# Angle tables by doubling, six accumulator blocks held in PSUM, and expert products placed by hand behind the scores, in a two-layer streaming encoder

## The chip, the core and the metric

One core of a Trainium2 chip runs the whole program. TensorE (PE in the profile, with PEld its weight loads) multiplies, VectorE (DVE), ScalarE (ACT) and GpSimd (POOL) do the rest, SyncE (SP) issues most transfers. The metric is the device time of one execution in microseconds, the median of several.

## What is computed

For 576 tokens (512 of a prompt, 64 of a sample) each of two layers does:

- three token mixers side by side: a diagonal complex state-space layer (SSM), banded attention, and retention; then gates, an output projection and a layer norm;
- PEER: for 8 heads, scores against 2 x 128 sub-keys, the best 16 of each, the best 16 of their sums; these name rows of two tables of 16384 experts,

```
u = u_tab[ek]                                  # 128 chosen experts of a token
act = gelu(einsum('bhkd,bd->bhk', u, xk))
w = gate * act
out = einsum('bhk,bhkd->bd', w, v_tab[ek])
```

- a gated input embedding and a further layer norm.

The SSM turns its state by angles that grow with the token: it needs tables of cos and sin of (t+1) times theta, 128 x 576 each, for 8 groups of states in each layer.

## The kernel before, in words

Activations lie with features on the partitions and tokens along the row. Every product of a weight block and activations is made of three matmuls, high part by high, high by low and low by high (`mm3_steps`, L215); `weights` (L207) loads a 128x1024 block `wr` from SP's queue, ACT casts it to `wh` (L204) and DVE, or POOL where `eng=G` is given, subtracts to get `wl` (L205). There are 3 buffers of `wr` and 4 each of `wh` and `wl`.

A planner that comes with the language orders the instructions of each engine by its own model of times, with the order of the program as the priority. Inside `manual_schedule(engines={PE})` PE alone keeps the order of the program. Each engine then works through its list in order, and so does SP's queue, stores among it.

PSUM has 8 banks: `lin` 3, `bgd` 1, `aux` (`bank()`) 4.

**Mixers** (`mixers`, L399). The SSM, retention, projections and gates are woven by hand-made estimates (`weave`, L137). `rotation` (L419) makes the angle tables on POOL: six products and sums over 128x576 from two small tables, `rot` (16 wide) and `rot16` (36 wide), which the start of the program fills by doubling on DVE. In layer 0 the SSM calls it for 8 groups (`begin`, L708). The tables of layer 1 are also made in layer 0, by `next_tables` (L919) in the attention, and are stored to DRAM on SP's queue (L922); layer 1 loads them. Up to `GB` = 8 gate tiles are made ahead as filling.

**PEER** (`peer_ple`, L994). 160 tokens are served by gathering rows (POOL's indirect loads L1237, DVE's L1243 and L1255). The other 416 are served densely: all 128 blocks of 128 experts are multiplied, and the weight of every pair that was not chosen is zero. The stages are:

1. Scores and top 16 (`query`, `top16`, to L1097).
2. The softmax (L1099 to L1106) and the list turns: five calls of `to_slots` (L1109), each five PE transposes and a copy by ACT. Then the key look-ups (L1157 to L1165): 32 rounds, each a mask by DVE and, for two halves, a matmul by PE and a predicated copy by DVE.
3. `FR0` = 128 steps of u products. `hidden(i)` (L1009) makes the products of block i in 8 steps of three 128x416 matmuls into a `lin` bank, and ACT puts the gelu into an `act` tile. The generator `prefetch` (L1017) does this for `N_EARLY` = 34 blocks spread over the 128, which are stored to DRAM, and for the first 8, which stay. The FR0 steps are the first ones under `manual_schedule`; in these POOL makes `wl`.
4. One-hot stage (L1198): in 26 rounds DVE makes one-hot matrices, PE sums the gates of each expert and token (L1210, L1211) and makes 8 more steps of u products, ACT writes `gs`, and SP stores it to `gd`.
5. Expert loop (L1283): 64 rounds of `GE` = 2 blocks. A round makes or reloads the u products of two blocks, `LA` = 6 blocks ahead of use; it multiplies two `act` tiles by the gates `gblk` (L1302, every fourth block on POOL, the others on DVE), splits them into Wh and Wl, converts two v blocks, and makes 6 matmuls for each of 8 output blocks d (L1324). For d < `HELD` = 2 the sum stays in PSUM over all rounds; for the other six it goes to an `aux` bank and DVE adds it to `R[d]` (L1329). Steps of the gathered part are spread over the rounds (`advance`).

Of the kernel before, what the change touches and what calls it, by code (L numbers as in the profile page):

```python
# [23 lines left out]
T = 576  # L24
TP = 512
# [24 lines left out]
N_EARLY = 34  # L50

GB = 8
# [10 lines left out]
FR0 = 128  # L63
# [5 lines left out]
GG = 4  # L69

HELD = 2
# [84 lines left out]
def body(ctx, tc, nc, A, O, depth=DEPTH, dbg=None):  # L156
# [156 lines left out]
    rot16 = [cst.tile([128, nst, 36], F32, name=f"rq{i}") for i in range(2)]  # L313
    with ExitStack() as c0:
# [58 lines left out]
        for i in range(2):  # L373
            V.memset(rot16[i][:, :, 0:1], 1.0 - i)
            V.tensor_copy(rot16[i][:, :, 1:2], rot[i][:, :, 15:16])
        for m in (1, 2, 4, 8, 16):
            double(V, rot16[0], rot16[1], 1, m)
        for i in range(2):
            V.tensor_copy(rot16[i][:, :, 32:36], rot16[i][:, :, 0:4])
# [19 lines left out]
def mixers(tc, env):  # L399
# [6 lines left out]
    with ExitStack() as c:  # L406
# [4 lines left out]
        o36 = lambda t: t.rearrange("p (a b) -> p a b", b=16)  # L411
# [7 lines left out]
        def rotation(qq, pl, bufs):  # L419

            new = lambda n, b=1: pl.tile([128, T], F32, name=n, bufs=b)
            ct, sn, tx = new("ct", bufs), new("sn", bufs), new("tx")
            c1 = [e.rot16[i][:, qq, :, None].to_broadcast([128, 36, 16]) for i in range(2)]
            c2 = [e.rot[i][:, qq, None, :].to_broadcast([128, 36, 16]) for i in range(2)]
            G.tensor_mul(o36(ct), c1[0], c2[0])
            G.tensor_mul(o36(tx), c1[1], c2[1])
            G.tensor_sub(ct, ct, tx)
            tx = new("tx")
            G.tensor_mul(o36(sn), c1[0], c2[1])
            G.tensor_mul(o36(tx), c1[1], c2[0])  # L430
            G.tensor_add(sn, sn, tx)
            return ct, sn
# [256 lines left out]
        def ssm():  # L689
# [18 lines left out]
            def begin(q):  # L708
# [4 lines left out]
                else:  # L713
                    ct, st = rotation(q, sp, 2)
# [114 lines left out]
        with ExitStack() as ca:  # L829
# [89 lines left out]
            def next_tables():  # L919
                for q in range(8):  # L920
                    for i, t in enumerate(rotation(L * 8 + 8 + q, pa, 1)):
                        SY.dma_start(e.tables[q, i], t)  # L922
                    yield
# [70 lines left out]
def peer_ple(tc, env):  # L994
# [8 lines left out]
    with ExitStack() as c:  # L1003
# [24 lines left out]
        fill = prefetch()  # L1028
        with ExitStack() as cr:
# [7 lines left out]
            with ExitStack() as ck:  # L1037
# [60 lines left out]

                ex = tk.tile([128, 5, 8, 16], F32, name="ex")  # L1099
# [9 lines left out]
                def to_slots(src, dst):  # L1109
# [5 lines left out]
                    S.copy(dst[:, TP:], p1[:, :64])  # L1115

# [40 lines left out]
                for dst, src, pos in ((IT, LT[0], aT), (JT, LT[1], bT)):  # L1157
                    V.memset(dst, 0.0)
                    for a in range(16):
                        mk = tk.tile([128, T], U16, name="mk", bufs=2)  # L1160
                        V.tensor_scalar(mk, pos, float(a), None, op0=OP.is_equal)
                        for lo, hi in HALF:
                            p = bank()
                            PE.matmul(p[:, :HF], sel[:, a], src[:, lo:hi], start=True, stop=True)
                            V.copy_predicated(dst[:, lo:hi], mk[:, lo:hi], p[:, :HF])  # L1165
                twice(I2, IT)
# [26 lines left out]
            man = ExitStack()  # L1193
# [270 lines left out]
```

## Time and profile before

| | us |
|---|---|
| median of 3 runs (4280.81, 4293.08, 4308.05) | 4293.08 |
| the profiled execution | 4261.82 |
| its span, first to last instruction | 4260.0 |
| granted TensorE clock, share of full | 0.974 |

A row of a view of stretches reads: start:end, its length, then for each engine its busy time and (x) the number of instructions begun, then the share of the clock that was granted, the mean busy share of the 16 DMA engines, and GB/s. A row of grouped instructions reads: line, engine, operation, out<-in, shapes, xcount | busy us, mean ns of one | idle time before them and what ended it. A row of waits reads: who waited <- for whom: us in total, times, the longest.

### The profile page before, as it was taken

What the parts mean: (1) busy time and instruction counts of PE and PEld (TensorE: products, weight loads), DVE (VectorE), ACT (ScalarE), POOL (GpSimd) and SP (SyncE); (2) the same over time, 40 slices, a digit from 0 to 9 for tenths busy, and PEclk for the clock granted to TensorE, in tenths of its full rate; (3) what the DMA queues carried; (4) which work ended last, traced back from release to release, by engine and by line L of the source; (5) the groups of instructions that cost most, each with busy time, mean ns of one, the idle gap of its engine ahead of it and who ended that gap; (6) DMA issues with size and microseconds to landing.
All of it is one profiled execution on the core that took longest, in us unless ns stands there. A gap on an engine that the chain in (4) does not pass through costs nothing.

```text
span 4260.0 us, 65840 instructions
## 1 busy us (share of the span) xinstructions
PE 4050.0 (95%) x25032; PEld 3789.8 (89%) x25032; DVE 3433.5 (81%) x6827; ACT 1562.5 (37%) x2600; POOL 1435.8 (34%) x1050
## 2 busy tenths in 40 slices
PE   6998999898999999999999999999989999999998
PEld 6787899798999999999787889897989999999997
DVE  8944459987999989999678344698979999999985
ACT  3223433376333333333432243333843333233324
POOL 4634123301545445443100011332035444454421
PEclk8999999999999999999999999999999999999999
DMA  3123222277998989898232222124789999889961
GB/s 114 56 76 113 67 72 79 96 262 266 321 336 315 330 297 331 302 336 283 68 99 83 83 85 78 60 81 137 282 287 331 322 327 317 311 310 321 320 210 43
DMA packets 353886, 873.78 MB, mean 205 GB/s; under 512 B 33184, under 2 KB 169504, under 8 KB 350240
## 3 DMA queue, kind: packets, MB, share of 16 engines
q1 hardware_dynamic: 261408, 533.98, 36.4%
q0 software_dynamic: 92160, 335.59, 22.1%
q8 instruction: 196, 3.21, 0.3%
q14 instruction: 122, 1.00, 0.1%
HBM read 788.09 MB, written 79.00 MB: 204 GB/s over the span
## 4 chain that ended last, share of the span: by engine, by line
PE 71%; DVE 15%; DMA 7%; POOL 3%; issue 2%; ACT 1%; SPq 0%; POOLq 0%; DVEq 0%; ACTq 0%
PE lin L221 38%; PE aux L1324 16%; DMA wr<-in_uT 3%; PE lin L1324 3%; PE bgd L1324 3%; PE aux L221 2%; PE aux L132 2%; DVE wl L205 1%; DVE s L1052 1%; DVE t L132 1%; PE aux L265 1%; PE aux L1210 1%; PE aux L1211 1%; DMA gr<-in_u,gidx 1%; DVE hi L132 1%
## 5 line engine op out<-in xcount | busy, mean ns | idle before, releaser
L221 PE MATMUL lin<-XH,wh 128*128 128x288 f32 (+1 forms) x4288 | 1411.9, 330 | 25.1 <-ACT wh L204 13.7
L221 PE MATMUL lin<-XH,wl 128*128 128x288 f32 (+1 forms) x4288 | 1392.8, 325 | 9.5 <-DVE wl L205 9.5
L221 PE MATMUL lin<-XL,wh 128*128 128x288 f32 (+1 forms) x4288 | 1396.3, 326 | 0.0
L204 ACT CAST wh<-wr 128x1024 fp32r<-128x1024 f32 x692 | 713.0, 1047 | 1861.8 <-PE aux L1324 675.6
L205 DVE TENSOR_TENSOR wl<-wr,wh 128x1024 fp32r<-128x1024 f32 x628 | 784.0, 1264 | 379.8 <-ACT wh L204 309.1
L221 PEld LDWEIGHTS lin<-XH,wh 128*128 128x128 f32 x4288 | 815.3, 190 | 65.2 <-issue 29.2
L221 PEld LDWEIGHTS lin<-XH,wl 128*128 128x128 f32 x4288 | 814.4, 190 | 18.3 <-DVE wl L205 10.5
L221 PEld LDWEIGHTS lin<-XL,wh 128*128 128x128 f32 x4288 | 815.7, 190 | 12.1 <-issue 7.3
L1324 PE MATMUL aux<-Wh,wh 128*128 128x416 f32 (+1 forms) x1560 | 552.0, 354 | 36.1 <-DVE R L1329 36.1
L1324 PE MATMUL aux<-Wh,wl 128*128 128x416 f32 (+1 forms) x1560 | 550.0, 353 | 0.0
L1237 POOL DMA_INDIRECT gr<-in_v,gidx x320 | 426.7, 1333 | 364.7 <-DVE gr L1243 215.4
L1237 POOL DMA_INDIRECT gr<-in_u,gidx x320 | 414.5, 1295 | 374.2 <-DVE acc L1255 214.5
L1329 DVE TENSOR_TENSOR R<-R,aux 128x416 f32<-128x416 f32 x780 | 426.0, 571 | 18.5 <-PE aux L1324 17.1
L1255 DVE SCALAR_TENSOR_TENSOR acc<-gr,wg,acc 128x1024 f32<-128x1024 f32 x316 | 407.6, 1290 | 12.1 <-DMA gr<-in_v,gidx 12.0
L1243 DVE SCALAR_TENSOR_TENSOR gr<-gr,xtok 128x1024 f32<-128x1024 f32 x320 | 406.1, 1272 | 10.0 <-DMA gr<-in_u,gidx 9.9
L1324 PEld LDWEIGHTS aux<-Wh,wh 128*128 128x128 f32 x1560 | 295.7, 190 | 45.8 <-DVE R L1329 45.2
L1302 POOL TENSOR_TENSOR act<-act,gblk 128x416 f32<-128x416 f32 x64 | 96.4, 1507 | 636.5 <-DMA gblk<-gd 453.2
L1324 PEld LDWEIGHTS aux<-Wh,wl 128*128 128x128 f32 x1560 | 295.8, 190 | 3.7
L1324 PE MATMUL aux<-gr,wh 128*128 128x416 f32 x780 | 272.8, 350 | 0.0
L1324 PE MATMUL aux<-Wl,wh 128*128 128x416 f32 x780 | 272.1, 349 | 0.0
L205 POOL TENSOR_TENSOR wl<-wr,wh 128x1024 fp32r<-128x1024 f32 x64 | 155.5, 2430 | 323.0 <-ACT wh L204 272.6
L1212 ACT ACTIVATE gs<-aux 128x512 f32<-128x512 f32 x208 | 206.7, 1166 | 0.0
(405 smaller groups left out, 5937.2 us busy)
## 6 DMA issues: line engine op xcount, KB each, us to landing
wr<-in_uT SPq DMA_DIRECT2D x256, 512.0 KB
wr<-in_v SPq DMA_DIRECT2D x256, 512.0 KB
gd<-gs SPq DMA_DIRECT2D x26, 2048.0 KB
gblk<-gd SPq DMA_DIRECT2D x64, 832.0 KB
wr<-in_w_in SPq DMA_DIRECT2D x92, 512.0 KB
wr<-in_peer_wq SPq DMA_DIRECT2D x32, 512.0 KB
ad<-act SPq DMA_DIRECT2D x68, 208.0 KB
act<-ad SPq DMA_DIRECT2D x68, 208.0 KB
```

The source lines that it names most:

```text
L132: return f(out, *a, **k)
L204: S.copy(hi, src)
L205: (eng or V).tensor_sub(lo, src, hi)
L221: PE.matmul(out[:, :b - a], wt[:, s], x[:, a:b], start=(first and k == 0 and g == 0), stop=(last and k == n - 1 and g == 2))
L265: PE.matmul(var[:1, :HF], ones1, sq, start=(d == 0), stop=(d == ND - 1))
L1212: S.activation(gs[:, :, o + t:o + t + 4].rearrange("p i t -> p t i"), p.rearrange("p (t i) -> p t i", t=4), AF.Copy, scale=1.0 / GSCALE)
L1237: G.indirect_dma_start(out=r, out_offset=None, in_=A[table], in_offset=bass.IndirectOffsetOnAxis(ap=gidx[:, s:s + 1], axis=0))
L1243: V.scalar_tensor_tensor(r, r, 1.0, xtok[s // 128], op0=OP.mult, op1=OP.mult, accum_out=dots[:, s:s + 1])
L1255: V.scalar_tensor_tensor(o, r, w, o, op0=OP.mult, op1=OP.add)
L1302: (G if GG and i % GG == 0 else V).tensor_mul(a3, a3, gblk[:, :, i % IB])
L1324: PE.matmul(p, x[:, w], y[:, a - NG:b - NG], start=(j == 0 and g == 0 and (e0 == 0 or not hold)), stop=(j == GE - 1 and g == 2 and (fin or ...
L1329: V.tensor_add(R[d][:, a:b], R[d][:, a:b], p)
```

## The change

- `rot16` goes. `rotation` starts from `rot` and doubles: for m = 16, 32, 64, 128, 256 ACT makes two products of m columns with a scale, and DVE two combined multiply-adds that write the next m columns; two copies of 16 and two of 64 columns by ACT complete a pair of tables.
- `GB` is 10; `N_EARLY` is 38.
- PE keeps the order of the program from the last scores on. `FR0` goes; 48 steps of u products (`FH`) stand behind the scores, 4 (`FS`) behind each list turn, 1 behind each half of a look-up.
- `HELD` is 6: `bgd`, two `lin` and three `aux` banks hold d = 0 to 5 over the whole loop; one `lin` bank is left for u products and one `aux` bank for d = 6 and 7. These two are copied to SBUF by ACT, and DVE adds the copy.
- A round's order is d = 0, 1, 2, 6, 3, 4, 5, 7, its first u block ahead of it and its second before d = 3.
- All gate products (L1302) are on DVE.

```diff
-N_EARLY = 34
-GB = 8
+N_EARLY = 38
+GB = 10
-FR0 = 128
+FH = 48
+FS = 4
-GG = 4
-HELD = 2
+HELD = 6
+ORDER = (0, 1, 2, 6, 3, 4, 5, 7)
...
-        for i in range(2):
-            V.memset(rot16[i][:, :, 0:1], 1.0 - i)
-            V.tensor_copy(rot16[i][:, :, 1:2], rot[i][:, :, 15:16])
-        for m in (1, 2, 4, 8, 16):
-            double(V, rot16[0], rot16[1], 1, m)
-        for i in range(2):
-            V.tensor_copy(rot16[i][:, :, 32:36], rot16[i][:, :, 0:4])
...
-            G.tensor_mul(o36(ct), c1[0], c2[0])
-            G.tensor_mul(o36(tx), c1[1], c2[1])
-            G.tensor_sub(ct, ct, tx)
-            tx = new("tx")
-            G.tensor_mul(o36(sn), c1[0], c2[1])
-            G.tensor_mul(o36(tx), c1[1], c2[0])
-            G.tensor_add(sn, sn, tx)
+            c0, s0 = (r[:, qq] for r in e.rot)
+            S.copy(ct[:, :16], c0)
+            S.copy(sn[:, :16], s0)
+            m = 16
+            while m < TP:
+                c, s = (c0, s0) if m == 16 else (ct[:, :m], sn[:, :m])
+                cm, sm = c[:, m - 1:m], s[:, m - 1:m]
+                S.activation(tx[:, 0, :m], s, AF.Copy, scale=sm)
+                S.activation(tx[:, 1, :m], c, AF.Copy, scale=sm)
+                V.scalar_tensor_tensor(ct[:, m:2 * m], c, cm, tx[:, 0, :m], op0=OP.mult, op1=OP.subtract)
+                V.scalar_tensor_tensor(sn[:, m:2 * m], s, cm, tx[:, 1, :m], op0=OP.mult, op1=OP.add)
+                m *= 2
+            for t in (ct, sn):
+                S.copy(t[:, TP:], t[:, :T - TP])
...
+                man.enter_context(tc.manual_schedule(engines={mybir.EngineType.PE}))
+                run(fill, FH)
                 ex = tk.tile([128, 5, 8, 16], F32, name="ex")
...
                     S.copy(dst[:, TP:], p1[:, :64])
+                    run(fill, FS)
...
                             V.copy_predicated(dst[:, lo:hi], mk[:, lo:hi], p[:, :HF])
+                            run(fill, 1)
...
-            man = ExitStack()
-            man.enter_context(tc.manual_schedule(engines={mybir.EngineType.PE}))
-            run(fill, FR0)
...
-            for i in range(e1, min(e1 + GE, 128)):
-                if i in acts:
-                    continue
-                if i in early:
-                    acts[i] = ap_.tile([128, ND_T], F32, name="act", bufs=LA + GE)
-                    SY.dma_start(acts[i], ad[i])
-                else:
-                    run(hidden(i))
+            ahead = iter([i for i in range(e1, min(e1 + GE, 128)) if i not in acts])
+            def first_products(n):
+                for _, i in zip(range(n), ahead):
+                    if i in early:
+                        acts[i] = ap_.tile([128, ND_T], F32, name="act", bufs=LA + GE)
+                        SY.dma_start(acts[i], ad[i])
+                    else:
+                        run(hidden(i))
             e0 = e1 - LA
             if e0 < 0:
+                first_products(GE)
                 continue
+            first_products(1)
...
-                (G if GG and i % GG == 0 else V).tensor_mul(a3, a3, gblk[:, :, i % IB])
+                V.tensor_mul(a3, a3, gblk[:, :, i % IB])
...
-                held = [e.bgd(), lin()][:HELD]
+                held = [e.bgd(), lin(), lin(), bank(), bank(), bank()]
...
-                for d in range(ND):
+                for d in ORDER:
+                    if d == 3:
+                        first_products(GE)
...
+                    if not hold:
+                        t = lp.tile([128, ND_T], F32, name="vo", bufs=2)[:, :b - a]
+                        S.copy(t, p)
+                        p = t
                     V.tensor_add(R[d][:, a:b], R[d][:, a:b], p)
```

## Rows read from the trace of the kernel before

**Rows 1.** The page's first part: busy time of each engine.
```profile
PE 4050.0 (95%) x25032; PEld 3789.8 (89%) x25032; DVE 3433.5 (81%) x6827; ACT 1562.5 (37%) x2600; POOL 1435.8 (34%) x1050
```
**Rows 2.** Stretches: one-hot stage, gap, both expert loops, 50 us of the first.
```profile
863.00:1025.50 162.50, 162.50 (x1434) 155.81 (x1432) 140.08 (x120) 134.05 (x153) 0.00 (x0) 1.00 0.70 263
1025.50:1042.40 16.90, 0.11 (x2) 0.00 (x0) 5.90 (x9) 8.33 (x14) 1.83 (x2) 0.57 0.77 257
1042.40:2044.00 1001.60, 984.05 (x5187) 969.00 (x5188) 945.58 (x1319) 311.02 (x436) 470.21 (x351) 0.99 0.89 312
3136.90:4137.00 1000.10, 981.25 (x5186) 967.31 (x5187) 945.90 (x1319) 311.06 (x436) 463.85 (x351) 0.99 0.89 312
1450.00:1500.00 50.00, 50.00 (x266) 49.41 (x265) 49.09 (x68) 15.68 (x23) 23.84 (x18) 1.00 0.92 324
```
**Rows 3.** Waits of PE in the first expert loop.
```profile
PE aux L1324 <- DVE R L1329: 17.3, 12, 5.1
```
**Rows 4.** Waits of PE in the second expert loop.
```profile
PE aux L1324 <- DVE R L1329: 18.8, 12, 5.2
```
**Rows 5.** Grouped instructions of DVE in the first expert loop.
```profile
L205 DVE TENSOR_TENSOR wl<-wr,wh 128x1024 fp32r<-128x1024 f32 x212 | 253.7, 1218 | 33.2 <-ACT wh L204 32.3 <-PE aux L1324 0.5 <-issue 0.2
L1329 DVE TENSOR_TENSOR R<-R,aux 128x416 f32<-128x416 f32 (+2 forms) x389 | 212.6, 572 | 9.5 <-PE aux L1324 9.0
...
L1302 DVE TENSOR_TENSOR act<-act,gblk 128x416 f32<-128x416 f32 x96 | 57.4, 608 | 0.0
```
**Rows 6.** Grouped instructions of ACT in the first expert loop.
```profile
L1014 ACT ACTIVATE act<-lin 128x416 f32<-128x416 f32 x86 | 43.8, 509 | 0.0
L1246 ACT ACTIVATE wg<-dots 128x16 f32<-128x16 f32 x10 | 2.1, 213 | 20.8 <-DVE gr L1243 20.8
```
**Rows 7.** Stretches of the mixers: layer 0 SSM, turnover, attention; layer 1 SSM, turnover.
```profile
34.00:281.00 247.00, 214.05 (x1292) 173.54 (x1292) 199.91 (x294) 58.86 (x123) 125.36 (x50) 0.91 0.19 60
281.00:351.50 70.50, 54.85 (x401) 53.66 (x399) 17.17 (x11) 15.41 (x29) 65.71 (x52) 0.91 0.36 127
2185.00:2394.00 209.00, 197.56 (x1259) 162.37 (x1259) 154.38 (x267) 57.74 (x120) 4.89 (x3) 0.97 0.26 80
2394.00:2446.60 52.60, 52.60 (x400) 52.27 (x398) 11.98 (x11) 15.42 (x28) 2.03 (x4) 1.00 0.33 109
351.50:557.00 205.50, 203.56 (x1552) 182.72 (x1552) 93.50 (x280) 84.61 (x215) 31.87 (x34) 0.99 0.25 82
```
**Rows 8.** Grouped instructions of DVE, 0 to 420 us (layer 0).
```profile
L132 DVE TENSOR_TENSOR t<-sn,bu 128x576 f32<-128x576 f32 x16 | 16.9, 1061 | 8.6 <-POOL sn L431 8.0 <-ACT bu L704 0.6
```
**Rows 9.** The same of DVE, 2090 to 2450 us (layer 1).
```profile
L132 DVE TENSOR_TENSOR t<-sn,bu 128x576 f32<-128x576 f32 x16 | 12.0, 749 | 3.5 <-ACT bu L704 3.4
```
**Rows 10.** DVE in order of time, two of the small doublings at the start.
```profile
29.42 0.17 DVE L364 TENSOR_TENSOR s__206<-rq 128x16 f32<-128x16 f32 x1
...
40.55 0.42 DVE L364 TENSOR_TENSOR s__206<-rq 128x256 f32<-128x256 f32 x1
```
**Rows 11.** Waits of SP's own queue, 281 to 351.5 us.
```profile
SPq L922 <- POOL sn L431: 25.8, 7, 4.3
SPq L922 <- POOL ct L427: 24.8, 7, 4.3
```
**Rows 12.** PE in order of time: the first list turn of layer 0.
```profile
786.70 1.41 PE L1113 MATMUL aux<-ident,ex 128*128 128x128 f32 x5 [4.12 <-DVE ex L1105]
```
**Rows 13.** u products of PE alone, look-up stage of layer 0 (busy of PE and PEld).
```profile
797.00:833.20 36.20, 33.66 (x131) 22.54 (x132) 1.00 0.31 101
```
**Rows 14.** DVE in order of time: the first one-hot of layer 0.
```profile
841.50 1.23 DVE L1187 TENSOR_TENSOR eJ<-iota,J 128x2048 f16<-128x2048 f16 x1 [2.59 <-DMA iota<-in_c_iota]
```
**Rows 15.** Waits of ACT in the first expert loop, for landings.
```profile
ACT wh L204 <- DMA wr<-in_v: 51.3, 17, 8.1
ACT wh L204 <- DMA wr<-in_uT: 48.6, 10, 9.7
```
**Rows 16.** ACT in order of time: two v blocks' casts in the first loop.
```profile
1330.17 2.00 ACT L204 CAST wh<-wr 128x1024 fp32r<-128x1024 f32 x2 [9.73 <-PE aux L1324]
```

More of the change, by code (lines that the diff above doesn't have):

```diff
@@ L312, in body @@
     rot = [cst.tile([128, nst, 16], F32, name=f"rot{i}") for i in range(2)]
-    rot16 = [cst.tile([128, nst, 36], F32, name=f"rq{i}") for i in range(2)]
     with ExitStack() as c0:
@@ L410, in mixers @@
         M = []
-        o36 = lambda t: t.rearrange("p (a b) -> p a b", b=16)
         def col(blk):
@@ L417, in mixers, with rotation @@
         gates = {}
[L419 to L424, printed above, removed]
-            G.tensor_mul(o36(ct), c1[0], c2[0])
-            G.tensor_mul(o36(tx), c1[1], c2[1])
-            G.tensor_sub(ct, ct, tx)
-            tx = new("tx")
-            G.tensor_mul(o36(sn), c1[0], c2[1])
-            G.tensor_mul(o36(tx), c1[1], c2[0])
-            G.tensor_add(sn, sn, tx)
+        def rotation(V, qq, pl, bufs):
+            ct, sn = (pl.tile([128, T], F32, name=n, bufs=bufs) for n in ("ct", "sn"))
+            tx = pl.tile([128, 2, 256], F32, name="tx")
+            c0, s0 = (r[:, qq] for r in e.rot)
[12 more added lines that the diff above has]
+                S.copy(t[:, TP:], t[:, :T - TP])
             return ct, sn
@@ L713, in begin @@
                 else:
-                    ct, st = rotation(q, sp, 2)
+                    ct, st = rotation(V, q, sp, 2)
                 if q % 2 == 0:
@@ L920, in next_tables @@
                 for q in range(8):
-                    for i, t in enumerate(rotation(L * 8 + 8 + q, pa, 1)):
+                    for i, t in enumerate(rotation(V, L * 8 + 8 + q, pa, 1)):
                         SY.dma_start(e.tables[q, i], t)
@@ L1028, in peer_ple @@
         fill = prefetch()
+        man = ExitStack()
         with ExitStack() as cr:
```

## The prediction

> **What bounds the kernel now.** I read the page's busy times first: PE is busy 95% of the span and DVE 81% [rows 1], so PE is the engine to save, and the stages must tell where DVE holds it. Next the stretches. The two expert loops take 1001.6 and 1000.1 us, 47% of the span. In 50 us of the first without a stall PE is busy throughout and begins 266 matmuls: 50/266 = 0.188 us for one of 416 columns [rows 2]. DVE is busy 945.6 of 1001.6 us there, and the reader should see that nothing else is near: ACT 311, POOL 470 [rows 2]. So the loop is PE's work with DVE just behind it. Third, the waits of PE in the loops: apart from a fraction of a microsecond all are for DVE's add to R, which has to empty an `aux` bank: 17.3 and 18.8 us, 12 each, up to 5 us [rows 3, 4]. The granted clock over the loops is 0.99 of full [rows 2]; what lies below full is time at the lower level, 1.2 GHz, after such stalls: 1% of the clock is about 20 us at half speed, 10 us lost (the row is rounded, so 5 to 15). Between one-hot stage and loop PE stands still for 16.9 us [rows 2], waiting for the first Wh. In the one-hot stage PE is busy 162.5 of 162.5 us.
>
> Fourth, layer 0 against layer 1 in the mixers, since only layer 0 makes tables. The SSM stretch takes 247 us with DVE busy 199.9 and POOL 125.4, against 209, 154.4 and 4.9 in layer 1; the turnover to attention takes 70.5 against 52.6 us, for the same 400 matmuls [rows 7]. Two mechanisms show. DVE's 576-column products take 1061 ns beside POOL and 749 without it [rows 8, 9]. And in the turnover SP's in-order queue waits 25.8 + 24.8 us for POOL's tables to store them [rows 11], with weight loads behind those stores.
>
> **The expert loops.** Four more u blocks are made ahead, 4 x 24 = 96 matmuls: 96 x 0.188 = 18.0 us less PE work in each loop; their loads of 512 KB move to before the loop, and 208 KB reloads replace them, which costs the loop no bandwidth.
>
> The adds: before, 6 x 63 rounds and 16 in the last, 394; after, 2 x 63 + 16 = 142. DVE saves 252 x 0.572 = 144 us [rows 5]. It takes over 32 gate products at 0.608 = 19 us and loses four `wl` at 1.218 = 5 us. From 946 it falls to about 816 us, 85% of a loop of 960. ACT gets 130 copies out of PSUM; not shown as such, the nearest is the gelu out of the same bank shape, 0.509 us [rows 6]: 66 us onto 311, below 40%. A first gate product of four now waits for its `gblk` in DVE's order, with `wl` and gathers queued behind it; DVE's 15% are the cover, and I cost it at nothing (else up to a few us a round in which `gblk` is late).
>
> So the wait for R loses its cause. What is late next: v blocks' `wl`, and the landings. I take two thirds of the stall (17.3 + 10 and 18.8 + 10 us, clock included) as gone: 18 and 19. Bounds: nothing gone, 18.0 us a loop; all gone, 46. Value: 36 and 37, loops of about 965 us.
>
> **From the scores to the loop.** Work that PE did in the planner's order is now in the program's. 48 steps are 48 x 3 x 0.188 = 27 us from 758 on, a little more if the clock is low at first, say 788, where the first turn ran at 786.7 after an idle 4.1 us [rows 12]. Each of the five turns is then followed by 12 matmuls, 2.25 us, and takes about 1 itself: look-ups from about 804 instead of 797. In the look-ups 131 u matmuls (24.6 us) and 64 short ones shared 36.2 us [rows 13], so a short one costs at most (36.2 - 24.6)/64 = 0.18, and 0.14 without the waits. Now each half carries three u matmuls: 64 x (0.56 + 0.14) = 45 us. The look-ups end at about 850 instead of 833, and DVE's first one-hot, 841.5 before [rows 14], comes at about 858. Four such operations of 1.23 us or a little more must end before the first matmul, say 7 us: 865. Before, PE itself was late: it came to the first one-hot matmul at 863 [rows 2]. Now PE will be early, and wait. So +2 us, with 132 + 8 steps done instead of 128 + 8. Bounds: -8 (DVE not delayed, PE's idle 4.1 us and half-clock time all saved) to +8.
>
> Then 26 rounds of 8, in which PE stays the bound, unchanged. 46 blocks are 368 steps; 368 - 132 - 208 = 28 are left and run before the loop: 28 x 0.56 = 15.8 us, inside the gap of 16.9 us in which PE only waited for `gd` to be stored and read. They are free there, and the clock stays up. If those loads delay `gblk`, they cost what they delay; that is in the bound. So the 18 us leave each loop and reappear where PE stood idle.
>
> **Tables.** One pair by doubling: columns 16 to 256, twice. DVE's small ops take 0.17 us at 16 columns and 0.42 at 256 [rows 10]: (0.17 + 0.19 + 0.22 + 0.29 + 0.42) x 2 = 2.6 us. ACT between 0.213 at 16 and 0.509 at 416 columns [rows 6]: 2.75 + 0.9 for the copies = 3.7 us. Eight pairs in the SSM of layer 0 put 20.6 us on DVE, and take POOL's work, and with it the slow products, away. The floor is layer 1's stretch, 209 us, 38 less. The other end: the chain of a pair goes from ACT to DVE and back five times, and if nothing else runs meanwhile each pair costs 2.6 + 2.75; 8 x 5.35 = 43 on 209, with some 9 us for the constants that only layer 0 makes: 261, +14. I take 209 + 20 = 229, -18, since DVE has other work to put between (it is 81% busy there [rows 7]).
>
> In the turnover the stores still stand before the weight loads on SP, but a pair's chain is 2.6 + 3.7 = 6.3 us where POOL was 65.7 us busy for 8 pairs, 8.2 each. Bounds 0 to -17.9, the whole difference to layer 1. I take -10. If these eight pairs slide into attention, 30 us of ACT and 21 of DVE lie beside a PE that is busy 203.6 of 205.5 us, while the two are busy 84.6 and 93.5 [rows 7]: +3 for order (0 to +20). Two more gates as filling: the same work earlier, nothing.
>
> The Trainium skill ("SBUF — State Buffer", Who interferes with whom) says that a VectorE instruction with two SBUF inputs and a GpSimd instruction that reads SBUF exclude each other; the trace agrees (1061 against 749 ns [rows 8, 9]). By it alone all of the 38 us would come back; without it only the chain counts.
>
> **Sum.** Mixers -18 - 10 + 3 = -25; before the loops 2 x 2 = +4; loops -73. Together -94. The profiled execution took 4261.8, so 4168; it was 31.3 us below the median of the runs, 4293.1, so as a median 4199.
>
> **Rivals.**
>
> *Landings hold the loop (B).* DMA engines are 0.89 busy over the loop and 0.92 where PE never stalls [rows 2]; a shorter loop raises that. ACT waits 99.9 us a loop for v and u weights to land [rows 15]. For it: those waits stand whatever DVE does. Against it: the stall-free 50 us moved 324 GB/s, more than the loop's 312. Then only the moved blocks count: -25 + 4 - 36 = -57, 4236.
>
> *Two banks are too few (C), the slower one.* One `aux` and one `lin` bank must be emptied by ACT before PE can go on, 18 matmuls or 3.4 us apart where a u block is reloaded, 7.9 where one is made. ACT's two casts of v take 2.0 us in a run [rows 16], harmless; but ACT is in order, and behind a cast that waits for its landing the copy waits too. At the limit all 99.9 us a loop [rows 15] reach PE: -94 + 200 = +106, 4399. It decides from 47% of that waiting (94 of 200 us). For it: those waits are up to 9.7 us, longer than 7.9. Against: a u block whose load is late stops PE anyway, and the held blocks (36 matmuls, 6.8 us) need no emptying. The Trainium skill ("Perfetto Trace Analysis", Matmuls) wants independent groups rotated through different banks so that emptying one overlaps the next group; here six of eight leave the rotation. No row shows a wait for ACT to empty a bank so far.
>
> *The tables' chain paces layer 0 (D).* It ends at +14, 0 and +20 instead of -25: -94 + 59 = -35, 4258.
>
> *The change does nothing to the loop* would need DVE's load not to fall; the adds are counted out, so this is B.
>
> **Chances.** Forecast 0.64 (own range 4150 to 4240), B 0.17, D 0.11, C 0.08. All of the forecast's gains at their better ends would be -38 - 18 - 16 - 92 = -164, hardly all at once: low 4135. Above, D and half of C's way are near 4260: high 4262. One per cent, 43 us, is about what a measurement of this kernel can tell from no change. Below 4250: 0.63 of the forecast, 0.13 of B, 0.05 of D, 0.81. Within 1%: 0.01 + 0.04 + 0.05 + 0.02 = 0.12. Slower by more: 0.07.
>
> **What would show it.** Right: each loop about 965 us with DVE near 85% and no wait of PE for R above 9 us in all; u matmuls in the gap before the loop; SSM of layer 0 near 229 us with 576-column products at 750 ns; turnover near 60. Wrong: PE waiting in the loop for ACT's copies or for the gelu (C), for `wl` behind landings (B), or DVE idle in layer 0 waiting for ACT's products (D); a first one-hot matmul later than 870.

## The result, and the profile after

The changed kernel takes 4136.07 us (median of 4, 4133.72 to 4139.9), the kernel before 4293.99 (median of 4): ratio 0.9633, 95% interval 0.9601 to 0.9664, 158 us less; 94 were forecast. The profiled executions took 4261.82 and 4139.9, so 122 us of the difference can be looked up in the two traces; the other 36 are not in them, and the first experiment is about these.

The stretches of the changed kernel: SSM, turnover and attention of layer 0; SSM and turnover of layer 1 (columns as in [rows 2]).

```profile
33.30:279.50 246.20, 230.54 (x1388) 187.81 (x1388) 180.52 (x350) 89.80 (x236) 4.70 (x2) 0.91 0.21 65
279.50:320.40 40.90, 40.07 (x305) 39.65 (x303) 21.10 (x49) 26.65 (x80) 1.37 (x5) 1.00 0.50 172
320.40:524.50 204.10, 202.01 (x1553) 181.20 (x1553) 104.81 (x320) 98.25 (x269) 29.79 (x32) 1.00 0.26 87
2109.40:2324.80 215.40, 209.66 (x1354) 174.70 (x1354) 156.44 (x268) 60.89 (x126) 4.89 (x3) 0.98 0.27 83
2324.80:2364.80 40.00, 40.00 (x305) 39.67 (x303) 9.60 (x9) 11.99 (x23) 2.41 (x4) 1.00 0.35 116
```

Against [rows 7]: layer 0's SSM stretch is as long as before, but holds 96 matmuls more (two gates); its turnover fell from 70.5 to 40.9 us. Attention took 204.1 us against 205.5, so the 3 us that were forecast for the tables' place in it did not come. In layer 1, SSM and turnover together went from 261.6 to 255.4.

The same view of layer 0 from the last scores to the first one-hot matmul, of the one-hot stage, the gap and both expert loops:

```profile
725.30:824.60 99.30, 95.25 (x528) 79.78 (x529) 84.05 (x267) 34.02 (x52) 38.52 (x20) 0.99 0.43 139
824.60:989.70 165.10, 164.16 (x1433) 157.64 (x1433) 145.97 (x126) 131.84 (x152) 5.84 (x3) 0.99 0.77 277
989.70:1007.00 17.30, 16.02 (x85) 15.40 (x84) 9.13 (x13) 11.93 (x19) 0.00 (x0) 1.00 0.81 277
1007.00:1969.60 962.60, 956.18 (x5091) 944.25 (x5092) 820.27 (x1095) 363.36 (x559) 422.50 (x313) 1.00 0.90 321
3050.90:4015.90 965.00, 955.82 (x5090) 944.26 (x5091) 820.55 (x1095) 363.14 (x559) 422.45 (x313) 1.00 0.90 320
```

The loops fell by 39 and 35 us, with 96 matmuls fewer each and DVE at 820 us instead of 946 [rows 2]. In the gap PE now works for 16.0 of 17.3 us. What PE waits for in the first loop:

```profile
PE bgd L1328 <- DVE wl L205: 5.8, 5, 2.5
PE bgd L1328 <- ACT Wh L204: 1.3, 1, 1.3
```

The waits for R of [rows 3] are gone, and in the second loop there is none either. A second wait went with them: ACT waited 48.6 us for u weights to land in the first loop before [rows 15], and waits 1.8 us for them here. What DVE waits for in the same loop matters below:

```profile
DVE wl L205 <- ACT wh L204: 56.0, 54, 5.8
DVE act L1304 <- DMA act<-ad: 49.8, 18, 4.7
```

### The profile page after: what moved, and what is told of

It reads as the page before. It is cut to its first block, busy times and chain, and to the rows that moved or that the text cites. A ratio compares the mean times of both kernels' runs of the same rounds, so it can differ in the third digit from the quotient of the medians.

```text
span 4138.1 us, 65747 instructions
## 1 busy us (share of the span) xinstructions
PE 4025.8 (97%) x25032; PEld 3768.2 (91%) x25032; DVE 3175.9 (77%) x6509; ACT 1728.5 (42%) x3084; POOL 1184.2 (29%) x892
## 4 chain that ended last, share of the span: by engine, by line
PE 80%; DVE 12%; DMA 2%; issue 2%; ACT 2%; POOL 1%; SPq 0%; POOLq 0%; DVEq 0%; ACTq 0%
PE lin L221 42%; PE aux L1328 16%; PE lin L1328 7%; PE bgd L1328 3%; PE aux L132 2%; PE aux L221 2%; DMA act<-ad 1%; PE aux L1208 1%; PE aux L1209 1%; PE aux L265 1%; DVE wl L205 1%; DVE s L1049 1%; DVE t L132 1%; DVE IX L1051 1%; DVE IX L1047 1%
## 5 line engine op out<-in xcount | busy, mean ns | idle before, releaser
L1235 POOL DMA_INDIRECT gr<-in_u,gidx x320 | 440.2, 1376 | 879.0 <-DVE acc L1253 386.1
L1328 PE MATMUL aux<-Wh,wl 128*128 128x416 f32 (+1 forms) x1300 | 453.7, 349 | 0.0
L1328 PE MATMUL aux<-Wh,wh 128*128 128x416 f32 (+1 forms) x1300 | 453.2, 349 | 0.0
L1241 DVE SCALAR_TENSOR_TENSOR gr<-gr,xtok 128x1024 f32<-128x1024 f32 x320 | 388.6, 1218 | 2.9 <-DMA gr<-in_u,gidx 2.9
L1335 ACT COPY vo<-aux 128x416 f32<-128x416 f32 x260 | 129.0, 496 | 363.7 <-PE aux L1328 357.2
L1328 PEld LDWEIGHTS aux<-Wh,wl 128*128 128x128 f32 x1300 | 244.1, 188 | 2.7
L1328 PEld LDWEIGHTS aux<-Wh,wh 128*128 128x128 f32 x1300 | 244.1, 188 | 1.1
L1210 ACT ACTIVATE gs<-aux 128x512 f32<-128x512 f32 x208 | 205.5, 1157 | 56.8 <-PE aux L1209 35.3
L1304 DVE TENSOR_TENSOR act<-act,gblk 128x416 f32<-128x416 f32 x256 | 147.0, 584 | 103.4 <-DMA act<-ad 102.8
L1328 PE MATMUL aux<-gr,wh 128*128 128x416 f32 (+2 forms) x650 | 226.0, 348 | 0.0
L1328 PE MATMUL aux<-Wl,wh 128*128 128x416 f32 (+2 forms) x650 | 225.9, 348 | 0.0
```

The costliest lines, as they stand in the source:

```text
L1210: S.activation(gs[:, :, o + t:o + t + 4].rearrange("p i t -> p t i"), p.rearrange("p (t i) -> p t i", t=4), AF.Copy, scale=1.0 / GSCALE)
L1235: G.indirect_dma_start(out=r, out_offset=None, in_=A[table], in_offset=bass.IndirectOffsetOnAxis(ap=gidx[:, s:s + 1], axis=0))
L1241: V.scalar_tensor_tensor(r, r, 1.0, xtok[s // 128], op0=OP.mult, op1=OP.mult, accum_out=dots[:, s:s + 1])
L1304: V.tensor_mul(a3, a3, gblk[:, :, i % IB])
L1328: PE.matmul(p, x[:, w], y[:, a - NG:b - NG], start=(j == 0 and g == 0 and (e0 == 0 or not hold)), stop=(j == GE - 1 and g == 2 and (fin or ...
L1335: S.copy(t, p)
```

## The experiments

| kernel | median us | ratio to before, 95% interval |
|---|---|---|
| before, again (e1) | 4287.54 | 1.0003 (0.9989 to 1.0017) |
| changed, 8 gates (e2) | 4156.34 | 0.9707 (0.9688 to 0.9727) |
| as e2, tables on POOL (e3) | 4209.56 | 0.9829 (0.9809 to 0.9849) |
| changed, old place of the u products (e4) | 4156.5 | 0.9707 (0.9687 to 0.9728) |
| changed, 34 early blocks (e5) | 4166.4 | 0.9707 (0.9672 to 0.9741) |
| changed, two blocks held (e6) | 4132.93 | 0.9638 (0.9604 to 0.9672) |
| changed, no copy by ACT (e7) | 4171.97 | 0.9725 (0.9696 to 0.9754) |
| changed, order 0 to 7 (e8) | 4213.76 | 0.9819 (0.9791 to 0.9848) |
| before, with the copy by ACT (e9) | 4342.78 | 1.0133 (1.0098 to 1.0167) |
| changed, 11 gates (e10) | 4139.17 | 0.9651 (0.9625 to 0.9677) |
| as e7, no wait for reloads (e11) | 4178.38 | 0.9759 (0.9725 to 0.9793) |
| changed, again (e12) | 4138.88 | 0.9659 (0.9633 to 0.9684) |

Each ratio goes by runs of the kernel before made beside it, whose medians lie between 4286.63 and 4293.99. So a few microseconds between two rows of the table say nothing. "Slower" below is the median less the changed kernel's 4136.07, where nothing else is named.

**The kernel before once more (e1).** No edit.

> The kernel before, once more, unchanged, for another profiled execution: the first one was 31 us below the median of its ordinary executions, while the changed kernel's profiled execution lies within 4 us of its median. Theory S (stalls that vary): the kernel before is near a balance of PE and DVE in the expert loops, and in some executions more of its waits for R last long enough that the granted clock falls; then a profiled execution near 4290 has loops of 1010 us or more, a loop clock below 0.99, and mixers that are the same within 3 us. Rival K (a constant offset of the first profile): all stages longer in proportion, or the profiled execution again near 4262 with the same stages within 3 us each. Median 4280 to 4300 in either case.

This profiled execution took 4297.89 us. Against the first one, the SSM stretches are 11 (layer 0) and 13.6 us longer, the loops 4 and 8; all else is the same within 1.3 us. So theory S holds in its kind, but I had put it into the wrong stage: most of it, 25 of 36 us, is in the mixers. The end of layer 1's SSM stretch in pieces of 15 us, first the execution of 4261.82:

```profile
2320.00:2335.00 15.00, 9.04 (x50) 5.67 (x48) 13.00 (x25) 0.98 (x4) 0.00 (x0) 0.77 0.05 14
2335.00:2350.00 15.00, 13.62 (x77) 9.83 (x77) 10.22 (x24) 4.35 (x8) 2.42 (x1) 1.00 0.19 62
2350.00:2365.00 15.00, 15.00 (x76) 9.32 (x74) 4.41 (x12) 2.08 (x6) 0.00 (x0) 1.00 0.11 31
```

and the one of 4297.89, the same kernel:

```profile
2335.00:2350.00 15.00, 9.03 (x44) 5.50 (x44) 14.23 (x29) 0.62 (x2) 0.00 (x0) 0.79 0.07 19
2350.00:2365.00 15.00, 13.63 (x73) 9.71 (x69) 7.64 (x19) 4.02 (x8) 2.42 (x1) 0.84 0.12 41
2365.00:2380.00 15.00, 15.00 (x37) 7.50 (x36) 4.19 (x9) 0.68 (x1) 0.00 (x0) 0.50 0.17 52
2380.00:2395.00 15.00, 15.00 (x68) 9.97 (x68) 3.61 (x10) 2.58 (x7) 0.00 (x0) 0.84 0.01 4
```

Read the first number behind the length, PE's busy time, and the third from the end, the clock. In both PE stands still for 6 us in the first piece. In the one it is back at full clock at once; in the other it is at 0.50, the lower level of 1.2 GHz, throughout a whole piece and partly in its neighbours: 37 matmuls in 15 us instead of 76, with PE busy all the time. A busy share alone would not show that.

**Eight gates (e2).**

```diff
-GB = 10
+GB = 8
```

> The changed kernel with 8 gates made as filling in the SSM stretch instead of 10; all else as changed. Theory G: the two more gates fill time in which PE stood idle or at half clock in the SSM stretch, so without them the SSM stretch of layer 0 goes from 246 to about 238 to 242 and its turnover from 41 to 53, and layer 1 goes back to 209 and 52.7; together 10 to 16 us slower, 4146 to 4152. Rival N (my forecast's term: the same work earlier, nothing): 4136 within 3 us, the SSM stretch of layer 0 shorter by the whole 12.6 us.

20 us slower in the median, beyond both theories; 15 between the profiled executions, within theory G's 10 to 16. In layer 1, SSM and turnover go back to 261.7 us, 6 more than with ten gates, and PE's 6 us stall is back, as expected. Layer 0's two stretches add up to 286.1 against 287.1, where nothing is lost; most of the other 9 us lie in the loops and the end, where the code is the same. So layer 1's part is shown, and why the median moves by 20 is not. That an exposed stall brings the clock's fall of e1 with it in some executions would add to it, but this execution does not show the fall.

**Tables on POOL (e3).** The old `rotation` and `rot16` with eight gates, compared with e2.

```diff
+            G.tensor_mul(o36(ct), c1[0], c2[0])
...
+            G.tensor_add(sn, sn, tx)
-                S.activation(tx[:, 0, :m], s, AF.Copy, scale=sm)
...
```

> The changed kernel with 8 gates, as the run before it, and with the angle tables made on POOL again by the old products (its 4.5 KB of factors are the space of the two gates). To be compared with the run of 8 gates. Theory T: the tables by doubling give most of layer 0's gain; 576-column products of DVE in layer 0 go back to about 1060 ns, SP waits for POOL's tables come back, the turnover goes from 53 to about 70, and the SSM stretch grows by 0 to 10 us: 17 to 28 us slower than the run of 8 gates, all of it in layer 0, about 4165 to 4178. Rival G2 (the gates did it all, the tables are neutral): within 4 us of the run of 8 gates.

53 us slower in the median, double what I expected. In the trace of e3, SSM and turnover of layer 0, then the SSM stretch of layer 1:

```profile
34.00:280.40 246.40, 215.18 (x1292) 174.35 (x1292) 200.35 (x293) 58.63 (x122) 125.38 (x50) 0.91 0.19 60
280.40:350.60 70.20, 54.79 (x399) 53.63 (x397) 16.75 (x11) 15.35 (x28) 65.43 (x52) 0.89 0.38 127
2145.00:2366.10 221.10, 209.93 (x1259) 168.66 (x1259) 154.75 (x267) 57.71 (x120) 4.89 (x3) 0.91 0.25 76
```

and the same three of e2:

```profile
34.50:266.80 232.30, 215.97 (x1292) 172.46 (x1292) 177.05 (x349) 86.69 (x229) 4.55 (x2) 0.92 0.21 64
266.80:320.60 53.80, 52.05 (x393) 51.62 (x391) 27.36 (x67) 35.36 (x108) 2.34 (x5) 1.00 0.48 161
2114.40:2323.50 209.10, 197.82 (x1259) 162.48 (x1259) 154.47 (x267) 57.86 (x120) 4.89 (x3) 0.97 0.26 80
```

In these two executions the tables are worth 14 us in the SSM stretch and 16 in the turnover, where SP's waits for POOL's tables are back as expected (25.8 and 24.9 us). The 14 is the less certain: that stretch moved by 11 us between two executions of one kernel in e1. The 12 in layer 1's SSM stretch, which makes no tables, are the fall of the clock seen in e1 (0.91 against 0.97, the same number of matmuls). One execution of each kernel does not tell whether it falls more often in this one. These three make 42 us; the other 11 of the 53 I cannot place.

The 576-column product takes 1084 ns in layer 0 of e3 and 749 in e2, as in the rows of e3 and e2:

```profile
L132 DVE TENSOR_TENSOR t<-sn,bu 128x576 f32<-128x576 f32 x16 | 17.3, 1084 | 8.2 <-POOL sn L432 8.0 <-ACT bu L705 0.2
```

```profile
L132 DVE TENSOR_TENSOR t<-sn,bu 128x576 f32<-128x576 f32 x16 | 12.0, 749 | 4.0 <-ACT bu L700 4.0
```

That is what the Trainium skill ("SBUF — State Buffer", Who interferes with whom) says of DVE with two SBUF inputs beside GpSimd; but the 8 us for which this product also waits for POOL's table are in the same row, and the rule doesn't speak of them.

**The old place of the u products (e4).** 132 steps in one call behind the look-ups, where the planner spreads the turns and look-ups among them.

```diff
-                run(fill, FH)
-                    run(fill, FS)
-                            run(fill, 1)
+            man.enter_context(tc.manual_schedule(engines={mybir.EngineType.PE}))
+            run(fill, FH + 5 * FS + 64)
             by[0] = V
             nxt = onehot(0)
```

> The changed kernel with its 132 steps of u products handed over behind the look-ups again, all at once, so that the planner's order places the list turns and look-ups among them; 38 early blocks and the 28 steps in the gap stay. Theory P: the program's order is worth the 6 and 7 us that the time from scores to the first one-hot matmul fell by, so 10 to 15 us slower, 4146 to 4151, with an idle stretch of PE of about 4 us before the first list turn and half-clock time behind it. Rival Q (my forecast's term: the order costs 2 us a layer): 4 us faster, 4132.

20 us slower; theory P, and more than its 10 to 15. From the last scores to the first one-hot matmul, then the one-hot stage, in layer 0 of e4:

```profile
719.50:828.60 109.10, 99.62 (x527) 84.31 (x528) 95.92 (x267) 33.79 (x52) 45.61 (x22) 0.94 0.40 131
828.60:990.90 162.30, 162.30 (x1434) 155.90 (x1434) 139.67 (x120) 131.67 (x152) 0.00 (x0) 1.00 0.77 278
```

and what PE waits for most in the first of these:

```profile
PE aux L1110 <- DVE ex L1102: 3.9, 1, 3.9
PE aux L1161 <- DVE JT L1162: 3.5, 3, 1.6
```

From the same matmul on it is 98.8 us in the changed kernel (its row above begins 0.6 us earlier), for the same work, at a clock of 0.99 instead of 0.94. The one-hot stage gives 2.8 us back in e4: in the changed kernel PE comes early to the first one-hots and waits 3 us for them, as the prediction said, and here it does not. Layer 1 does the same (104.8 us against 98.8). That makes 11 us net; the rest of the median's 20 I cannot place (the first loop, the same code, was 7 us longer).

**34 early blocks (e5).**

```diff
-N_EARLY = 38
+N_EARLY = 34
```

> The changed kernel with 34 early u blocks instead of 38: four more are made inside each loop (96 matmuls), and the gap before the loop has no u steps. Theory M (PE's work sets the loop): each loop 18 us longer, about 980 and 983, the gap as long as now though PE is idle in it, the one-hot stages 2 us shorter: 4136 + 36 - 4 = 4168, and up to 6 more if the clock falls in the gap. Rival B (landings hold the loop): the loops stay within 3 us of 962 and 965, 4130 to 4140.

30 us slower; theory M, and B falls. Gap and loops:

```profile
980.70:997.60 16.90, 0.05 (x1) 0.05 (x1) 7.16 (x12) 8.55 (x14) 0.00 (x0) 0.60 0.77 255
997.60:1981.50 983.90, 975.38 (x5185) 963.32 (x5186) 824.09 (x1097) 367.67 (x565) 434.91 (x313) 1.00 0.89 314
3060.50:4045.80 985.30, 977.61 (x5185) 965.73 (x5186) 824.67 (x1097) 367.69 (x565) 430.97 (x313) 1.00 0.90 313
```

21.3 and 20.3 us a loop for 96 matmuls, and a gap of the same length in which PE does nothing. The two loops make 41.6 us, and the profiled executions differ by only 29, because layer 0's SSM and turnover took 278.5 us in this one against 287.1 in that of the changed kernel (e12 comes back to this).

**Two blocks held (e6).** Six blocks a round go through ACT's copy and DVE's add.

```diff
-HELD = 6
+HELD = 2
```

> The changed kernel with two v blocks held in PSUM instead of six; the other six go through ACT's copy and DVE's add in every round. Theory D (DVE's load makes the stalls): 252 more adds at 0.58 us put 147 us on DVE's 820, 967 in all, more than PE's 944 in the loop; loops of 985 to 1000 us with PE waiting for banks again, 4180 to 4210. Rival A (what counts is that ACT, not DVE, empties the bank): the copies free the banks in time whatever DVE does, loops within 5 us, 4136 to 4146.

No slower: rival A, and the step on which the prediction's second half rests falls. The two loops:

```profile
999.30:1958.00 958.70, 956.04 (x5089) 943.88 (x5090) 937.94 (x1347) 483.48 (x819) 469.96 (x313) 1.00 0.92 322
3041.80:4008.10 966.30, 957.99 (x5089) 943.34 (x5090) 936.78 (x1347) 482.80 (x819) 483.23 (x313) 1.00 0.92 320
```

and the adds among the grouped instructions of its first loop:

```profile
L1337 DVE TENSOR_TENSOR R<-R,vo 128x416 f32<-128x416 f32 (+2 forms) x389 | 220.1, 584 | 10.2 <-ACT vo L1335 9.5
```

DVE is busy 938 of 958.7 us, nearly as long as in the kernel before and in a shorter loop, and PE is busy 956 us of it; for a copy it waits 0.2 us.

**No copy by ACT (e7).** DVE adds the two free blocks straight from PSUM.

```diff
-                        t = lp.tile([128, ND_T], F32, name="vo", bufs=2)[:, :b - a]
-                        S.copy(t, p)
-                        p = t
```

> The changed kernel with six blocks held, but DVE adds the other two to R straight from PSUM, without ACT's copy. Theory D (DVE's load makes the stalls): at 85% DVE is early enough mostly; PE waits 2 to 6 us a loop for these adds, 4138 to 4148. Rival A (the copy by ACT is what frees the bank in time): waits of 15 us or more a loop as in the kernel before, 4166 or more.

36 us slower, with DVE busy 822 of 981 us: rival A again. The waits of PE in its first loop:

```profile
PE aux L1328 <- DVE R L1335: 19.5, 14, 2.9
```

As much as in [rows 3], at a lower load. One of them in order of time, first DVE's row of operations (start, length, idle time before):

```profile
1093.05 0.59 DVE L1304 TENSOR_TENSOR act<-act,gblk 128x416 f32<-128x416 f32 x1
1096.48 0.59 DVE L1304 TENSOR_TENSOR act<-act,gblk 128x416 f32<-128x416 f32 x1 [2.85 <-DMA act<-ad]
1096.99 0.58 DVE L1335 TENSOR_TENSOR R<-R,aux 128x416 f32<-128x416 f32 x1
```

and PE's:

```profile
1097.62 0.46 PE L1328 MATMUL aux<-Wh,wh 128*128 128x416 f32 x1 [2.92 <-DVE R L1335]
```

DVE isn't late because it is busy: it stands still for 2.85 us in front of a gate product whose reloaded `act` has not landed, and the add that would free PE's bank is next in its list. Eleven of the 14 waits, 18.6 of the 19.5 us, come like this, shortly after DVE stood still for 2.6 to 4.3 us for an `act<-ad`.

In the kernel before, the waits of [rows 3] look alike, but DVE stood in front of other operations. This is the longest of them, with ACT, DVE and PE in turn:

```profile
1564.61 1.04 ACT L204 CAST wh<-wr 128x1024 fp32r<-128x1024 f32 x1 [9.74 <-DMA wr<-in_uT]
1565.69 1.23 DVE L205 TENSOR_TENSOR wl<-wr,wh 128x1024 fp32r<-128x1024 f32 x1 [5.66 <-ACT wh L204]
1569.11 0.72 PE L1324 MATMUL aux<-Wh,wh 128*128 128x416 f32 x1 [5.07 <-DVE R L1329]
```

The weights of a u block landed late, so ACT's cast waited, so DVE's `wl` waited, and the adds stood behind it. Four waits make 13.2 of the 17.3 us; before each of them DVE had stood still for 2.6 to 5.7 us, three times so, once for a gathered row. In most of the shorter ones DVE was busy throughout, so its load of 94% of the loop had a small part. DVE's gate products waited for nothing there [rows 5].

So the two runs show one mechanism with two causes. In the changed kernel the late u weights are nearly gone with the copy (1.8 us) and without it (5.3 us in e7), and late reloads in front of DVE's gate products are new. e7 therefore shows what the copy is worth in the changed kernel. It does not show that the copy ended the waits of the kernel before; which part of the change lets the u weights land earlier was not tried.

**Order 0 to 7 (e8).** In the program the two free blocks come one right behind the other.

```diff
-ORDER = (0, 1, 2, 6, 3, 4, 5, 7)
+ORDER = (0, 1, 2, 3, 4, 5, 6, 7)
```

> The changed kernel with the v blocks in the order 0 to 7, so that the two that are not held come one right behind the other (now three held blocks lie between them). Theory C2 (one free aux bank has to be emptied by ACT before the next such block): 64 times a loop PE waits 0.5 to 0.9 us for the copy, 32 to 58 us a loop, 4200 to 4250, with waits of PE for ACT's copy in the loop. Rival R (the planner or the u products of the next round lie between): no such waits, 4132 to 4142.

78 us slower, 43 and 38 a loop (1005.7 and 1003.1): C2's price. The first loop and its longest waits, which are named otherwise than I expected:

```profile
997.90:2003.60 1005.70, 974.52 (x5088) 946.93 (x5089) 819.77 (x1095) 363.16 (x559) 400.19 (x313) 0.99 0.88 307
...
PE bgd L1328 <- DVE wl L205: 21.0, 15, 2.7
PE aux L1328 <- ACT vo L1335: 5.4, 3, 3.2
```

Mostly PE waits for the next v block's `wl`, not for the copy. Idle time is 25 us more than in the changed kernel; the other 18 of the 43 are PE's busy time, longer for the same matmuls at a clock of 0.99. `manual_schedule` ends behind the one-hot stage, so in the loop the planner orders PE's instructions too. It put three or four matmuls (of a u block, or of the next round's first v block) between the two free blocks, so even here they do not follow each other directly. The price of the order is shown, its path is not settled. The Trainium skill ("Perfetto Trace Analysis", Matmuls) wants independent groups to rotate through different banks. Here no run with the copy and three held blocks between two uses of the only free `aux` bank shows more than 0.4 us of waits for it, and the run without these blocks between is 40 us a loop slower.

**The kernel before with the copy (e9).** Two held, natural order, all else as before.

```diff
+                    if not hold:
+                        t = lp.tile([128, ND_T], F32, name="vo", bufs=2)[:, :b - a]
+                        S.copy(t, p)
+                        p = t
                     V.tensor_add(R[d][:, a:b], R[d][:, a:b], p)
```

> The kernel before with one change: the six v blocks that are not held are copied out of PSUM by ACT, and DVE adds the copy to R. Two blocks held, natural order, 34 early blocks, products on POOL as before. Theory H (what held PE was an add that stood in DVE's order behind an operation waiting for a landing; the copy takes the bank out of that order): the waits of PE for R, 17 to 25 us a loop, go, and each loop falls by 18 to 25 us to about 980 to 984: 4290 - 40 = 4250. Rival L (the load of DVE): no gain, 4280 to 4295.

A plain miss: 53 us slower than the kernel before, where I expected 40 faster; the loops take 1026.8 and 1027.7 us. What ACT waits for in its first loop, and what PE then waits for:

```profile
ACT vo L1331 <- DVE R L1333: 248.8, 141, 9.9
ACT wh L204 <- DMA wr<-in_v: 114.5, 28, 6.9
...
PE bgd L1324 <- DVE wl L205: 22.8, 28, 3.0
PE aux L1324 <- ACT vo L1331: 6.9, 8, 1.9
```

The wait for R is gone, as theory H had it, but the copy has two buffers, and DVE frees them. Six copies come close together, so ACT stands still behind DVE 141 times, and the casts of the next v block stand behind those copies. The head of the line has moved from DVE to ACT. In e6, which also copies six blocks a round, the same wait is 51.6 us: there u products lie between the blocks in most rounds, the gate products are on DVE, and four more blocks are made early. Which of these makes the difference was not tried.

**Eleven gates (e10).**

```diff
-GB = 10
+GB = 11
...
-                    ct, st = rotation(V, q, sp, 2)
+                    ct, st = rotation(V, q, sp, 2, wk("t3")[:, :512].rearrange("p (a b) -> p a b", b=256))
```

> The changed kernel with 11 gates as filling; the scratch of the table doubling in layer 0's SSM shares a work tile, which makes the space. Theory G (PE runs out of filling at about 199 us in layer 0, waits 6.0 us for DVE and then runs at half clock for a while, as layer 1 did with 8 gates and does not with 10): one gate of 6.3 us closes most of that wait; the SSM stretch of layer 0 stays near 237, its turnover falls by 6; 6 to 12 us faster than the changed kernel, 4124 to 4130. Rival T (DVE's chain is what paces the end of the SSM stretch, and sharing the scratch lengthens it): no gain or slower, 4136 to 4146.

No gain. In layer 0 the 6.0 us wait for `hr` fell to 1.7, and the turnover to 33.6; but the waits for `sd` grew from 3.1 to 5.0, and the SSM stretch took 245.8 us at a clock of 0.92. Its two stretches add up to 279.4 us, as in the quicker executions of the changed code (below): filling the one stall moved the loss.

**No wait for reloads (e11).** As e7, but the reload goes to a spare tile, so the output lacks the reloaded blocks.

```diff
-                        SY.dma_start(acts[i], ad[i])
+                        G.memset(acts[i], 0.0)
+                        SY.dma_start(lp.tile([128, ND_T], F32, name="spare", bufs=2), ad[i])
```

> As the run in which DVE adds straight from PSUM (e7), but the reloaded u products don't reach the gate product: the reloads of 208 KB go into a spare tile with the same traffic, and the product takes a tile of zeros, so the 38 early blocks are left out of the output. DVE's load is the same. Theory H (head of line): DVE no longer stands still in front of the product until the reload has landed, and the waits of PE for R fall from 19.5 us to under 8 us a loop: 4172 - 2 x 15 = about 4142. Rival L (load, or the bank's own latency): the waits stay near 19 us, 4165 to 4178.

The total says L, the trace says H. The first 110 us of its loop, and the next 866:

```profile
999.80:1110.00 110.20, 88.94 (x422) 85.98 (x423) 78.43 (x115) 28.16 (x40) 40.48 (x34) 0.89 0.92 321
1110.00:1976.00 866.00, 866.00 (x4609) 858.15 (x4607) 740.79 (x971) 276.95 (x389) 381.45 (x317) 1.00 0.90 315
```

against e7, the same two stretches:

```profile
999.80:1110.00 110.20, 107.14 (x564) 105.10 (x565) 101.08 (x146) 36.52 (x52) 53.55 (x41) 1.00 0.94 329
1110.00:1976.00 866.00, 849.40 (x4493) 836.90 (x4492) 718.66 (x945) 268.63 (x378) 344.37 (x273) 1.00 0.90 315
```

and what PE waits for in the second of these in e7 (in e11 no wait is listed there):

```profile
PE aux L1328 <- DVE R L1335: 16.6, 13, 2.3
```

From 110 us on PE in e11 is busy 866.00 of 866.00 us: without the reload in front of the product, adds straight from PSUM hold nothing, at the same load of DVE (86%, as in e7's 83%). At the start v blocks landed late (ACT waited up to 15.5 us, and PE once 7.7 us for R behind that), and 142 matmuls fewer were begun in 110 us than in e7. That start ate the gain. I take it for an effect of my edit, since nothing held the spare loads back any more; that is not shown.

**The changed kernel once more (e12).** No edit.

> The changed kernel once more, unchanged, beside the run with 11 gates on the same chip, and for another profiled execution: in its first one the SSM stretch of layer 0 took 246 us, in the runs of this study with the same code there 237 to 239. Theory S (the clock after a stall falls or not, by execution): 237 to 239 here with a granted clock of 0.94 or more, median 4132 to 4140. Rival K: 246 again, which would tie it to this program.

Median 4138.88, in the range given; but layer 0's SSM stretch took 243.8 us at a clock of 0.92, which is neither theory's number: it took 237 to 239 in e4 to e8 and e11, and 246 in the first. The same 6.0 us stall for `hr` is in all of these, so it is again the clock behind the stall; what decides is open.

## Why the prediction was right, and where its steps failed

The direction came out. The time lies only 1 us above the low end of the range, 4135, and below the forecast's own 4150 to 4240, and the sum came about in part by other ways; that the range held was in part luck. Each part by what taking it back costs in the median, beside its term:

| part | forecast | taken back |
|---|---|---|
| tables by doubling (e3 to e2) | -25 | -53 |
| two more gates (e2) | 0 | -20 |
| program's order behind the scores (e4) | +4 | -20 |
| four more early blocks (e5) | -36 | -30 |
| the stalls for R: copy (e7) | -37 | -36 |
| six held instead of two (e6) | in the line above | +3, nothing |

The five add up to 159 us, against 158 measured. That is chance: they are not independent (the order of the round alone, e8, is worth 78), and of the first three the traces place 42 of 53, 6 of 20 and 11 of 20 us.

*The early blocks.* Right in mechanism, and nearly in size: PE's work sets the loop, and the gap took it in. Rival B, held to be the next likely, falls with e5 (21 us a loop come back).

*The stalls.* The size was right (two thirds of 17 to 19 us and of the clock), the reason wrong. "So the wait for R loses its cause" followed from DVE's load falling from 946 to 816 us. The load fell to 820, and it did not matter: at 938 PE doesn't wait (e6), at 822 it waits 19.5 us (e7). What made the waits is the order in DVE's list: an add behind an operation that itself waits for a landing, directly (e7's rows, e11) or through ACT's cast (the rows of the kernel before under e7). The copy takes PE's bank out of that list. It did not pay everywhere: with the old order of the round the loops are as long as before (e8, 1005.7 against 1001.6 us), and in the kernel before it costs 53 us (e9). DVE's list does wait in front of gate products, though for the reloaded `act` (49.8 us) and not for `gblk` as the prediction feared; only no bank of PE hangs on it. What the prediction had no term for is the late u weights, from which most of the waits in the first loop of the kernel before came, and which went as well.

*Rival C* named the real danger (ACT's casts and copies in one list) at too high a price for this order: PE waits for no copy. Some of it comes about with six copies in a row, 53 us above the kernel before in e9.

*The tables.* The floor was taken from layer 1, 38 us less, and half of it given away to the chain. Rival D had the chain pace the layer: ACT's products and DVE's sums do wait for each other (12.5 us of ACT and 7.1 of DVE in the SSM stretch of the changed kernel), and a pair takes 4.6 us of ACT and 3.2 of DVE instead of 3.7 and 2.6, but SSM and turnover together still gained 30 us in e3's comparison against the 28 forecast (-18 and -10). The split was other than forecast (14 and 16), and the rest of the 53 lies outside of layer 0, 12 us of it behind a lower clock in layer 1, for which the prediction had no term.

*Two more gates, "nothing".* PE had a 6 us stall in layer 1's SSM stretch, within the 209 us that the prediction used as its floor. I looked only at sums there, and not for where PE stood.

*Program's order, +2 each.* The chain of DVE was not delayed: the first one-hot matmul comes 98.8 us after the first u product behind the scores, in the kernel before 104.8 (863.1 less 758.3). The bound of -8 had the reason right (idle and half-clock time saved), and I took the other end.

*From the profiled execution to the median.* I carried the 31.3 us between them over as a constant. By e1 they were mostly (25 of 36 us) time at a lower clock behind stalls in the SSM stretches, of which that first execution had been spared a part, and the change took some of the stalls away: its own profiled execution lies 4 us above its median. That step alone is 35 of the 63 us between forecast and result.

## What to carry to other kernels

Before an engine's load is blamed for a wait, look at what stands in front of the releasing instruction in that engine's list: an engine that stands idle there waits for something itself, and then less load does not help. Before a PSUM bank is given to another engine, look at what would stand in front of the copy in that engine's list, leave matmuls of other banks between two uses of the bank, and count the copy's buffers, since they can hand the wait on. When a profiled execution is a per cent off its median, compare a second one stage by stage before the difference is carried over.

## What the runs showed of the hardware that I had not expected

Behind the same 6.0 us stall of PE the granted clock was at full in the next piece of 15 us in some executions (the kernel before, e2) and lay at 0.50 for a whole 15 us in others (e1, e3), which made layer 1's SSM stretch 12 to 14 us longer for the same code. What decides between them stays open. DVE's add takes nearly as long from SBUF as from PSUM (584 ns in e6; 572 in [rows 5]), so the copy neither costs DVE time nor saves it any.
